# Feed-forward down projection by seven products of halves with weight low parts made by an adding DMA, and gate and up sums chained in PSUM

## The chip, the cores and the metric

The kernel runs on one core of a Trainium2 chip. The metric is the device time of one execution in microseconds (us); several executions are timed and their median is quoted. One execution is recorded by the hardware profiler, and the trace of it is what all rows below come from. Engine names are those of the profile: PE is the matrix engine, PEld its weight loads, DVE the vector engine, ACT the scalar engine, POOL the GpSimd engine, SP the engine that issues the loads.

## The reference, cut to what matters

One encoder layer over 512 tokens of width 1024: a feed-forward block (FFN1), attention and a short convolution with a combined input and an output projection, a second feed-forward block of the same shape (FFN2), and a gated embedding at the end. The change touches the two feed-forward blocks only. All values are float32.

```python
def swiglu(x, wg, wu, wd):
    return (jax.nn.silu(x @ wg) * (x @ wu)) @ wd
...
x = layer_norm(DN_ALPHA * x + 0.5 * swiglu(x, ffn1_wg[i], ffn1_wu[i], ffn1_wd[i]), ln1_g[i], ln1_b[i])
...
x = layer_norm(DN_ALPHA * x + 0.5 * swiglu(x, ffn2_wg[i], ffn2_wu[i], ffn2_wd[i]), ln3_g[i], ln3_b[i])
```

x is 512 x 1024, wg and wu are 1024 x 2816, wd is 2816 x 1024.

## The kernel before, in words

**Products of float32.** Each operand is held as two fp32r tiles, a high part (a rounding cast on ACT, L111) and a low part (the operand less its high part, a subtraction on DVE, L112); `split` makes both. A product is three matmul passes, high by high, high by low, low by high (`PASSES`), each recorded at L132 in `mm`. `unit` (L114) loads a 512 KB block of weights by an SP DMA into a page and splits it.

**Tiling of an FFN** (`ffn`, L239). The 2816 hidden columns are 22 chunks of 128. They are taken in groups of 4, 4, 4, 4 and 6 chunks. For each group the gate and up products of its chunks are computed, then silu(gate) x up (silu on ACT L329, product on DVE L330, into a tile hf), then the group's part of the down projection is added into `nat`, the 512 x 1024 result, four tiles of 128 tokens.

**Gate and up.** The first two chunks of an FFN go through `plain`. All others go two chunks at a time through `two` (L302): the 1024 x 256 block of each of wg and wu and the tokens are cut in halves, and seven products of halves (of sums of quarters: S1 to S4 of the weights, made by `weights` on DVE at L286, L287, L292, L293; T1 to T4 of the tokens, made once) give what eight would. Each of the seven products is 24 matmuls of 256 columns into a PSUM bank of its own (gate and up side by side, 512 columns). They are combined outside PSUM: one copy on ACT (L333) and seven sums of 512 columns on DVE (L334 to L342). `put_chunk` makes silu, hf and the split of hf for each of the two chunks.

**Down projection of a four-chunk group** (L389 to L399). For each of two column halves, four PSUM banks, one for each block of 128 tokens, take 4 chunks x 3 passes of 128 x 512; 96 matmuls in all. wd comes in four 512 KB blocks by `unit`. Eight `scalar_tensor_tensor` of 512 columns on DVE (L399) add the banks into `nat`. The last group of six chunks (L373 to L388) also does the layer norm; its form is left as it is by the change.

**What sets the order.** Each engine runs its instructions in one fixed order, made by a scheduler from the program order and from priorities: code under `tc.high_priority(offset=n)` is moved n places ahead. The offset is 25 for the first chunks of FFN1 and 100 for later ones, 400 and 50 in FFN2, 125 and 0 for wd. Working tiles live in a ring of 38 pages of 512 KB, handed out first freed, first reused (`page`, `free`); a tile that is written into a reused page waits for the last reader of the page's former tile. There are eight PSUM banks, handed out in turn.

## Time and profile before

| | us |
|---|---|
| median of three runs | 1027.2 |
| the three runs | 1023.98, 1028.66, 1027.2 |
| the profiled execution | 1026.09 |
| its span in the trace | 1024.0 |

The profiled execution is 1.1 us under the median and inside the three runs; its span leaves out 2.1 us at its two ends. Its mean granted clock of PE is 0.998 of full speed. FFN1 runs from about 11 to 320 us of the span and FFN2 from about 630 to 936 us; a four-chunk group takes 62 us. The rows below are of this execution: busy time of an engine is the union of its instructions, and an instruction's own duration is longer than the distance to the next one where they run back to back.

### The profile page before, as it was taken

To read this page: it belongs to the slowest core of one execution; us is meant where nothing else is said; L and a number is where in the kernel's file an instruction comes from. 1 tells how busy PE (TensorE), PEld (TensorE's weight loads), DVE (VectorE), ACT (ScalarE), POOL (GpSimd) and SP (SyncE) were. 2 spreads that over 40 slices of the span, in tenths; PEclk is the share of its full clock that TensorE was granted. 3 is DMA by queue.
4 is the path that set the end of the run, shared out by engine and by line. 5 is a ranking of instruction groups with operands and counts; after the bars stand their busy time and mean duration, and the time that the engine had idled before them with its cause. 6 is when DMAs were issued, how large, how long until landed. Compare 5 with 4: busy or idle time off the path is not lost.

```text
span 1024.0 us, 15507 instructions
## 1 busy us (share of the span) xinstructions
PE 1004.6 (98%) x6313; PEld 903.8 (88%) x6313; DVE 822.2 (80%) x1283; ACT 441.8 (43%) x621; POOL 25.0 (2%) x35
## 2 busy tenths in 40 slices
PE   8999999999999999999999999999999999999998
PEld 7989999898998878888878778989999898998787
DVE  7897868978697958999479988896868969689852
ACT  6444424433354235332576836443425324246221
POOL 1000000000000200000000011000000000000100
PEclk9999999999999999999999999999999999999999
DMA  9342324323335231424013223331424322227111
GB/s 311 122 123 83 109 98 131 97 83 107 100 119 185 69 92 42 128 58 124 20 42 104 83 65 101 124 124 39 127 83 144 103 79 87 83 85 265 52 41 51
DMA packets 99510, 104.57 MB, mean 102 GB/s; under 512 B 5872, under 2 KB 81904, under 8 KB 99440
## 3 DMA queue, kind: packets, MB, share of 16 engines
q1 hardware_dynamic: 99440, 103.60, 31.8%
q8 instruction: 49, 0.80, 0.3%
q14 instruction: 21, 0.17, 0.1%
HBM read 101.49 MB, written 2.10 MB: 101 GB/s over the span
## 4 chain that ended last, share of the span: by engine, by line
PE 89%; DMA 4%; DVE 3%; ACT 3%; issue 1%; POOLq 0%; SPq 0%; ACTq 0%
PE bk L132 86%; ACT pg L111 2%; DVE pg L112 1%; DMA pg<-in_ffn_wu_dram 1%; PE bk L506 1%; DMA pg<-in_w_in_dram 1%; DMA pg<-in_x_t_dram 1%; PE bk L507 1%; PE bk L704 1%; DMA pg<-in_ple_proj_w_dram 1%; DMA pg<-in_ffn_wd_dram 0%; PE bk L146 0%; ACT a L676 0%; DMA pg<-in_ple_gate_w_dram 0%; PE bk L692 0%
## 5 line engine op out<-in xcount | busy, mean ns | idle before, releaser
L132 PE MATMUL bk<-pg,pg 128*128 128x256 f32 (+1 forms) x2832 | 496.4, 333 | 4.4 <-ACT pg L111 1.8
L132 PEld LDWEIGHTS bk<-pg,pg 128*128 128x128 f32 x2832 | 427.6, 190 | 56.0 <-ACT pg L111 2.6
L111 ACT CAST pg<-pg 128x1024 fp32r<-128x1024 f32 (+1 forms) x267 | 260.0, 984 | 313.3 <-PE bk L132 78.4
L112 DVE TENSOR_TENSOR pg<-pg,pg 128x1024 fp32r<-128x1024 f32 (+1 forms) x267 | 300.6, 1139 | 40.6 <-ACT pg L111 35.5
L132 PE MATMUL bk<-xq,pg 128*128 128x256 f32 x2208 | 275.3, 284 | 4.6 <-DVE mv L158 1.5
L132 PEld LDWEIGHTS bk<-xq,pg 128*128 128x128 f32 x2208 | 270.6, 193 | 7.0 <-ACT pg L111 2.3
L132 PE MATMUL bk<-xT,pg 128*128 128x512 f32 (+2 forms) x600 | 133.0, 381 | 0.3 <-ACT xT L111 0.2
L132 PEld LDWEIGHTS bk<-xT,pg 128*128 128x128 f32 (+1 forms) x600 | 109.9, 186 | 21.5 <-ACT xT L111 0.5
L132 PE MATMUL bk<-pg,xT 128*128 128x512 f32 (+1 forms) x312 | 69.5, 374 | 1.3 <-DVE nat L385 1.3
L132 PEld LDWEIGHTS bk<-pg,xT 128*128 128x128 f32 x312 | 55.0, 188 | 11.4 <-ACT pg L111 1.8
L329 ACT ACTIVATE a<-pg 128x512 f32<-128x512 f32 x40 | 25.2, 629 | 71.7 <-DVE pg L338 66.1
L111 ACT CAST pg<-hf 128x512 fp32r<-128x512 f32 (+1 forms) x56 | 34.6, 618 | 35.2 <-DVE hf L330 19.6
L112 DVE TENSOR_TENSOR pg<-hf,pg 128x512 fp32r<-128x512 f32 (+1 forms) x56 | 38.3, 684 | 4.7 <-ACT pg L111 4.5
L399 DVE SCALAR_TENSOR_TENSOR nat<-bk,nat 128x512 f32<-128x512 f32 x64 | 40.4, 682 | 0.8 <-PE bk L132 0.7
L330 DVE TENSOR_TENSOR hf<-a,pg 128x512 f32<-128x512 f32 x40 | 27.5, 688 | 13.6 <-ACT a L329 13.5
L338 DVE TENSOR_TENSOR pg<-bk,pg 128x512 f32<-128x512 f32 x20 | 13.8, 692 | 29.9 <-PE bk L132 29.4
L160 POOL TENSOR_TENSOR mv<-mv,mhalf 128x1 f32<-128x1 f32 x12 | 17.8, 1480 | 627.0 <-DVE mv L159 627.0
L286 DVE TENSOR_TENSOR pg<-pg,pg 128x512 f32<-128x512 f32 x40 | 27.3, 686 | 5.7 <-DMA pg<-in_ffn_wg_dram 5.7
L292 DVE TENSOR_TENSOR pg<-pg 128x512 f32<-128x512 f32 x40 | 27.4, 686 | 2.9 <-PE bk L132 2.9
L112 DVE TENSOR_TENSOR pg<-bk,pg 128x512 fp32r<-128x512 f32 (+2 forms) x37 | 22.5, 626 | 8.5 <-ACT pg L111 8.1
L287 DVE TENSOR_TENSOR pg<-pg,pg 128x512 f32<-128x512 f32 x40 | 27.3, 685 | 0.0
L293 DVE TENSOR_TENSOR pg<-pg,pg 128x512 f32<-128x512 f32 x40 | 27.1, 686 | 0.1
(100 smaller groups left out, 612.7 us busy)
## 6 DMA issues: line engine op xcount, KB each, us to landing
pg<-in_ffn_wg_dram SPq DMA_DIRECT2D x44, 512.0 KB, 4.1
pg<-in_ffn_wu_dram SPq DMA_DIRECT2D x44, 512.0 KB, 4.7
pg<-in_ffn_wd_dram SPq DMA_DIRECT2D x44, 512.0 KB, 4.0
pg<-in_w_in_dram SPq DMA_DIRECT2D x28, 512.0 KB, 3.6
pg<-in_w_out_dram SPq DMA_DIRECT2D x8, 512.0 KB, 3.9
pg<-in_ple_gate_w_dram SPq DMA_DIRECT2D x8, 512.0 KB, 4.8
pg<-in_x_t_dram SPq DMA_DIRECT2D x4, 512.0 KB, 7.5
nat<-in_x_dram SPq DMA_DIRECT2D x4, 512.0 KB, 8.9
```

The costliest lines, as they stand in the source:

```text
L111: nc.scalar.copy(hi, src)
L112: nc.vector.tensor_sub(lo, src, hi.bitcast(F32))
L132: nc.tensor.matmul(ps, lhsT=st[a], rhs=mv[b], start=first and i == 0 and k == 0, stop=last and i == n - 1 and k == 2)
L160: nc.gpsimd.tensor_tensor(mv[:, 3:4], mv[:, 2:3], mhalf, op=ALU.pow)
L286: nc.vector.tensor_add(S1, A21, A22)
L287: nc.vector.tensor_sub(S2, S1, A11)
L292: nc.vector.tensor_sub(S3, A11, A21)
L293: nc.vector.tensor_sub(S4, A12, S2)
L329: nc.scalar.activation(s_t, e[m][:, :, 0], AF.Silu)
L330: nc.vector.tensor_mul(h3, s_t, e[m][:, :, 1])
L338: nc.vector.tensor_add(e[0][:, 1], prod("S4", "B22"), u4)
L399: nc.vector.scalar_tensor_tensor(dst, acc[t], CY, dst, op0=ALU.mult, op1=ALU.add)
```

## The change

Three things change, for the eight four-chunk groups (four in each FFN) and, for the second, for all twenty calls of `two`.

1. **Down projection by seven products** (`down7`). The hidden values of a pair of chunks are cut in halves by chunk and by tokens (256 columns), wd by chunk and by columns (512). `pair_ops` makes the four sums of quarters of the hidden values on DVE (four operations of 256 columns) and splits three of the four quarters (768 columns) and the sums (1024 columns) into high and low parts; the silu products are written straight into the tile `pair` and no longer split one by one. `diff` makes four sums of wd quarters (T1 to T4, 1024 columns each, DVE). Seven products over two token blocks, two pairs and three passes are 84 matmuls of 128 x 512. They go into three pairs of banks X, Y, Z; several products are summed in one bank, and each stage of a bank is added into `nat` by `put_out`, 14 operations of 512 columns a group.
2. **Weight parts** (`parts`). The high part of each of the seven wd operands is a cast on ACT. The low part is no longer a subtraction on DVE: ACT writes the operand times -1, rounded to fp32r, and a DMA issued by POOL adds the operand to it in place, 512 KB each. Loads of wd, parts and differences have priority 200 in both FFNs.
3. **Gate and up sums in PSUM** (`two`). The products are chained in three banks: b1 takes A11, then S2, S3 and A22 products on top, b2 takes A12, b3 takes S1, then S4. ACT copies the stages of b1 to SBUF (four copies of 512 columns), and three DVE sums remain.

```diff
@@ -248,7 +249,117 @@
+        SLOT = {"A12": 0, "A22": 1, "A11": 2, "A21": 3, "S1": 0, "S2": 1, "S3": 2, "S4": 3}
+        def raw_of(pair, m):
+            return pair[:, 2 - 2 * m:4 - 2 * m]
+        def pair_ops(pair):
+            A12, A22, A11, A21 = (pair[:, i] for i in range(4))
+            a = page([P, 4, 256]), page([P, 4, 256])
+            split(a[0][:, :3], a[1][:, :3], pair[:, :3])
+            s_ = page([P, 4, 256], F32)
+            nc.vector.tensor_add(s_[:, 0], A21, A22)
+            nc.vector.tensor_sub(s_[:, 1], s_[:, 0], A11)
+            nc.vector.tensor_sub(s_[:, 2], A11, A21)
+            nc.vector.tensor_sub(s_[:, 3], A12, s_[:, 1])
+            sums = page([P, 4, 256]), page([P, 4, 256])
+            split(*sums, s_)
+            free(pair, s_)
+            return a, sums
+        def down7(f0, pairs):
+            w4 = wd[f0 * P:(f0 + 4) * P].rearrange("(i k p) n -> k p i n", k=2, p=P)
+            hp = lambda: tc.high_priority(offset=AHEAD_W)
...
+            B11, B12, B21, B22 = (raw[i] for i in ((0, 0), (0, 1), (1, 0), (1, 1)))
+            def parts(src):
+                hi, lo = page([P, 2, 512]), page([P, 2, 512])
+                nc.scalar.copy(hi, src)
+                nc.scalar.mul(lo, src, -1.0)
+                nc.gpsimd.dma_start(lo, src, accum_op=ALU.add)
+                return hi, lo
+            def diff(a, b):
+                t = page([P, 2, 512], F32)
+                nc.vector.tensor_sub(t, a, b)
+                return t
+            def product(banks, a, w, first):
+                for b in range(2):
+                    for i, (q, sums) in enumerate(pairs):
+                        st = sums if a[0] == "S" else q
+                        for n, (x_, y_) in enumerate(PASSES):
+                            nc.tensor.matmul(banks[b], lhsT=st[x_][:, SLOT[a], ts(b)], rhs=w[y_][:, i],
+                                             start=first and i == 0 and n == 0, stop=i == 1 and n == 2,
+                                             skip_group_check=not first)
+            def put_out(banks, m, n):
+                for b in range(2):
+                    dst = nat[2 * m + b][:, n * 512:(n + 1) * 512]
+                    nc.vector.scalar_tensor_tensor(dst, banks[b], CY, dst, op0=ALU.mult, op1=ALU.add)
+            X_, Y_, Z_ = ([bank("all") for _ in range(2)] for _ in range(3))
+            with hp():
+                w = parts(B11)
+            product(X_, "A11", w, True)
+            put_out(X_, 0, 0)
+            free(*w)
...
+            with hp():
+                T1 = diff(B12, B11)
+                w = parts(T1)
+                free(B11)
+            product(Y_, "S1", w, True)
+            put_out(Y_, 1, 1)
+            free(*w)
...
@@ -299,7 +408,7 @@
+            def product(ps, a, b, first):
                 for i, (nm, _) in enumerate(mats):
-                    mm(ps[:, i], [((W[nm][a][0][:, c], W[nm][a][1][:, c]), (X.q[b][0][:, c], X.q[b][1][:, c])) for c in range(4)])
+                    for c in range(4):
+                        for k, (x_, y_) in enumerate(PASSES):
+                            nc.tensor.matmul(ps[:, i], lhsT=W[nm][a][x_][:, c], rhs=X.q[b][y_][:, c],
+                                             start=first and i == 0 and c == 0 and k == 0,
+                                             stop=i == 1 and c == 3 and k == 2, skip_group_check=not first)
                 return ps
...
-            nc.scalar.copy(p1, prod("A11", "B11"))
-            nc.vector.tensor_add(e[0][:, 0], prod("A12", "B21"), p1)
-            nc.vector.tensor_add(u2, prod("S2", "T2"), p1)
-            p5 = prod("S1", "T1")
-            nc.vector.tensor_add(u4, p5, u2)
-            nc.vector.tensor_add(e[0][:, 1], prod("S4", "B22"), u4)
+            b1, b2, b3 = bank2(), bank2(), bank2()
+            nc.scalar.copy(p1, product(b1, "A11", "B11", True))
+            nc.vector.tensor_add(e[0][:, 0], product(b2, "A12", "B21", True), p1)
+            nc.scalar.copy(u2, product(b1, "S2", "T2", False))
+            product(b3, "S1", "T1", True)
+            nc.scalar.copy(u3, product(b1, "S3", "T3", False))
+            nc.vector.tensor_add(e[1][:, 1], b3, u3)
+            nc.vector.tensor_add(e[0][:, 1], product(b3, "S4", "B22", False), u2)
             put_chunk(0)
-            nc.vector.tensor_add(u3, prod("S3", "T3"), u2)
-            nc.vector.tensor_add(e[1][:, 1], p5, u3)
-            nc.vector.tensor_add(e[1][:, 0], prod("A22", "T4"), u3)
+            nc.scalar.copy(e[1][:, 0], product(b1, "A22", "T4", False))
             put_chunk(1)
...
@@ -386,18 +503,9 @@
             else:
-                for half in range(2):
-                    acc = [bank("all") for _ in range(NTB)]
-                    for i in range(per):
-                        wv = wd_rows(i, half)
-                        for t in range(NTB):
-                            mm(acc[t], [(both(h[i], ts(t)), wv)], first=i == 0, last=i == per - 1)
-                        free(*held[i, half])
-                    for t in range(NTB):
-                        dst = nat[t][:, half * 512:(half + 1) * 512]
-                        nc.vector.scalar_tensor_tensor(dst, acc[t], CY, dst, op0=ALU.mult, op1=ALU.add)
-            free(*h)
+                down7(f0, h[::2])
```

The places left out are the loads of the four quarters of wd, five more products of the same form in `down7`, and the callers.

**How it moves instructions.** The rows are the engines' orders in the third group of FFN1 (`[waits X]` is a wait on engine or queue X; DMAHW are queues of loads, DMASW those of POOL's DMAs). First ACT of the kernel before, from the copy of the second `two` of the group to the split of its third chunk: pg17, pg16 and pg31 are high parts of wd, pg13 and pg2 those of hf.

```order
L333 COPY pg14_188_1691<-bk_49_1693 128x512 [waits PE_49]
L329 ACTIVATE a_9_1633<-pg35_159_1439 128x512 [waits DVE_49]
L111 CAST pg17_193_1896<-pg7_192_1894 128x1024 [waits DMAHW5_49]
L111 CAST pg16_199_1964<-pg32_198_1962 128x1024 [waits DMAHW6_49]
L111 CAST pg13_163_1636<-hf_9_1632 128x512 [waits DVE_49]
L111 CAST pg31_202_1994<-pg10_201_1992 128x1024 [waits DMAHW7_49]
L329 ACTIVATE a_10_1824<-pg8_186_1689 128x512 [waits DVE_49,Activation_49]
L111 CAST pg2_190_1827<-hf_10_1823 128x512 [waits DVE_49]
```

Now ACT at the same place after the change, from the middle of the second `two` to the cast of the second pair's three quarters (the last row). L289 and L291 are the high part and the times -1 of `parts`, L441 silu, L453 the last copy of bank b1.

```order
L289 CAST pg12_251_2035<-pg0_250_2033 128x1024 [waits DVE_49]
L289 CAST pg27_245_1993<-pg10_244_1991 128x1024 [waits PE_49]
L291 ACTIVATE pg9_246_1994<-pg10_244_1991 128x1024 [waits PE_49]
L289 CAST pg28_248_2014<-pg5_247_2012 128x1024 [waits PE_49]
L291 ACTIVATE pg20_249_2015<-pg5_247_2012 128x1024 [waits PE_49]
L291 ACTIVATE pg30_252_2036<-pg0_250_2033 128x1024
L289 CAST pg32_253_2054<-pg36_239_1945 128x1024 [waits DMAHW7_49]
L441 ACTIVATE a_10_1895<-pg31_227_1738 128x512 [waits DVE_49]
L453 COPY pg29_228_1739<-bk_29_1742 128x512
L441 ACTIVATE a_11_1923<-pg29_228_1739 128x512 [waits Activation_49]
L291 ACTIVATE pg31_254_2055<-pg36_239_1945 128x1024 [waits DVE_49]
L112 CAST pg35_231_1926<-pg13_204_1687 128x768 [waits DVE_49]
```

Two wd casts of 1024 columns stood between a silu and the next cast that the matmuls read; now there are eight operations of `parts` among these twelve, two more of them right ahead, all in front of the cast of the second pair.

PE of the kernel before, from the last matmul of gate and up into the down projection: bk_56 to bk_59 are its first four banks.

```order
L132 MATMUL bk_55_1857<-pg26_26_355,pg3_177_1666 128x256
L132 MATMUL bk_56_1890<-pg17_193_1896,pg0_162_1576 128x512 [waits PE_49,Activation_49]
L132 MATMUL bk_56_1890<-pg30_194_1897,pg0_162_1576 128x512 [waits DVE_49]
L132 MATMUL bk_56_1890<-pg17_193_1896,pg0_162_1576 128x512
L132 MATMUL bk_57_1891<-pg17_193_1896,pg0_162_1576 128x512 [waits PE_49]
L132 MATMUL bk_57_1891<-pg30_194_1897,pg0_162_1576 128x512
```

PE after the change, inside the down projection of the same group, from the first S1 product to the first A11 matmul of the second pair (pg35, the tile that the last ACT row above writes).

```order
L305 MATMUL bk_34_1949<-pg27_245_1993,pg11_202_1683 128x512 [waits Activation_49]
L305 MATMUL bk_35_1950<-pg27_245_1993,pg11_202_1683 128x512
L305 MATMUL bk_34_1949<-pg9_246_1994,pg11_202_1683 128x512 [waits DMASW0_49]
L305 MATMUL bk_34_1949<-pg27_245_1993,pg19_203_1684 128x512
L305 MATMUL bk_35_1950<-pg9_246_1994,pg11_202_1683 128x512
L305 MATMUL bk_35_1950<-pg27_245_1993,pg19_203_1684 128x512
L305 MATMUL bk_37_1952<-pg17_242_1972,pg8_199_1674 128x512 [waits PE_49,Activation_49]
L305 MATMUL bk_37_1952<-pg1_243_1973,pg8_199_1674 128x512
L305 MATMUL bk_37_1952<-pg17_242_1972,pg33_200_1675 128x512
L305 MATMUL bk_32_1947<-pg4_240_1953,pg35_231_1926 128x512 [waits Activation_49]
```

Before, a down projection began when both chunks' splits were there and waited on ACT and DVE at its head; now its matmuls wait for ACT's parts, for the adding DMAs (DMASW), for a bank that ACT copies out, and for the second pair's cast.

## Rows read from the trace of the kernel before

**Rows 1.** The page's busy times by engine, share of the span, instructions.
```profile
PE 1004.6 (98%) x6313; PEld 903.8 (88%) x6313; DVE 822.2 (80%) x1283; ACT 441.8 (43%) x621; POOL 25.0 (2%) x35
```

**Rows 2.** The chain that ended last: start us, us, engine, tile, line, count.
```profile
11.04 308.99 PE bk L132 x2219
629.88 305.84 PE bk L132 x2201
```

**Rows 3.** Three group lengths of FFN1: busy by engine, clock, DMA share, GB/s.
```profile
core 0: us, PE busy (x) PEld busy (x) DVE busy (x) ACT busy (x) POOL busy (x), PEclk, DMA share, GB/s
62.00:124.00 62.00, 62.00 (x433) 58.26 (x432) 50.70 (x69) 24.93 (x31) 0.00 (x0) 1.00 0.32 102
124.00:186.00 62.00, 62.00 (x434) 58.23 (x433) 48.72 (x65) 24.50 (x30) 0.00 (x0) 1.00 0.31 103
186.00:248.00 62.00, 62.00 (x433) 58.27 (x432) 50.31 (x69) 24.73 (x31) 0.00 (x0) 1.00 0.31 102
```

**Rows 4.** PE's timeline into the first down projection: start us, us, instructions.
```profile
42.75 5.92 PE L132 MATMUL bk<-xq,pg 128*128 128x256 f32 x48
48.51 27.71 PE L132 MATMUL bk<-pg,pg 128*128 128x256 f32 x144
76.06 4.12 PE L132 MATMUL bk<-xq,pg 128*128 128x256 f32 x33
```

**Rows 5.** Groups by line and form: count, busy us, mean ns, idle before.
```profile
L112 DVE TENSOR_TENSOR pg<-pg,pg 128x1024 fp32r<-128x1024 f32 x226 | 273.5, 1221 | 37.7 <-ACT pg L111 33.0 <-ACT a L329 2.7 <-PE bk L132 1.7
L111 ACT CAST pg<-pg 128x1024 fp32r<-128x1024 f32 x226 | 235.8, 1050 | 270.3 <-PE bk L132 63.4 <-DVE pg L287 56.4 <-DMA pg<-in_ffn_wd_dram 47.3
L399 DVE SCALAR_TENSOR_TENSOR nat<-bk,nat 128x512 f32<-128x512 f32 x64 | 40.4, 682 | 0.8 <-PE bk L132 0.7
L330 DVE TENSOR_TENSOR hf<-a,pg 128x512 f32<-128x512 f32 x40 | 27.5, 688 | 13.6 <-ACT a L329 13.5
L329 ACT ACTIVATE a<-pg 128x512 f32<-128x512 f32 x40 | 25.2, 629 | 71.7 <-DVE pg L338 66.1 <-DVE pg L342 5.6
L333 ACT COPY pg<-bk 128x512 f32<-128x512 f32 x20 | 11.7, 586 | 14.7 <-PE bk L132 14.6
L112 DVE TENSOR_TENSOR pg<-bk,pg 128x256 fp32r<-128x256 f32 x8 | 3.3, 414 | 0.0
```

**Rows 6.** ACT's timeline in the fourth group of FFN1, columns as in rows 4.
```profile
225.12 0.63 ACT L329 ACTIVATE a<-pg 128x512 f32<-128x512 f32 x1 [0.16 <-DVE pg L342]
225.65 2.02 ACT L111 CAST pg<-pg 128x1024 fp32r<-128x1024 f32 x2
227.57 0.62 ACT L111 CAST pg<-hf 128x512 fp32r<-128x512 f32 x1
```

**Rows 7.** DVE's timeline in the same group, columns as in rows 4.
```profile
229.86 2.35 DVE L112 TENSOR_TENSOR pg<-pg,pg 128x1024 fp32r<-128x1024 f32 x2
...
254.42 1.28 DVE L399 SCALAR_TENSOR_TENSOR nat<-bk,nat 128x512 f32<-128x512 f32 x2
255.68 1.23 DVE L112 TENSOR_TENSOR pg<-pg,pg 128x1024 fp32r<-128x1024 f32 x1
```

**Rows 8.** DMA issues: count, KB each, median us from issue to landing.
```profile
pg<-in_ffn_wd_dram SPq DMA_DIRECT2D x44, 512.0 KB, 4.0
...
nat<-in_x_dram SPq DMA_DIRECT2D x4, 512.0 KB, 8.9
out_dram<-hf SPq DMA_DIRECT2D x7, 256.0 KB, 2.0
```

**Rows 9.** DMA queues: packets, MB, share of 16 engines.
```profile
q1 hardware_dynamic: 99440, 103.60, 31.8%
```

**Rows 10.** A stretch in which PE waits, columns as in rows 3.
```profile
328.00:330.00 2.00, 0.98 (x6) 0.48 (x4) 1.29 (x2) 1.89 (x3) 0.76 (x1) 1.00 0.00 0
```

**Rows 11.** POOL's costliest group, columns as in rows 5.
```profile
L160 POOL TENSOR_TENSOR mv<-mv,mhalf 128x1 f32<-128x1 f32 x12 | 17.8, 1480 | 627.0 <-DVE mv L159 627.0
```

More of the change, by code (lines that the diff above doesn't have):

```diff
@@ L37 @@
 AHEAD_D2 = 0
+AHEAD_W = 200
 NEMB = 2
@@ L262, in plain @@
                 free(*u)
-            hf = ring("hf", 2, [P, 512])
             s_t = ring("a", 2, [P, 512])
             nc.scalar.activation(s_t, ps["g"], AF.Silu)
-            nc.vector.tensor_mul(hf, s_t, ps["u"])
-            return put(hf)
+            nc.vector.tensor_mul(hf, s_t.rearrange("p (a b) -> p a b", a=2), ps["u"].rearrange("p (a b) -> p a b", a=2))
         def weights(w, fc, ops, pages):
@@ L300, in weights, with two @@
             yield
-        def two(fc, ah):
+        def two(fc, ah, place):
             W, pages = {nm: {} for nm, _ in mats}, []
@@ L320, in two, with bank2 @@
+            def bank2():
+                return bank("all").rearrange("p (m n) -> p m n", m=2)
             e = [page([P, 2, 2, 256], F32) for _ in range(2)]
             k = [page([P, 2, 2, 256], F32) for _ in range(2)]
-            p1, u2, u3, u4 = k[0][:, 0], k[0][:, 1], k[1][:, 0], k[1][:, 1]
-            h = []
+            p1, u2, u3 = k[0][:, 0], k[0][:, 1], k[1][:, 0]
             def put_chunk(m):
-                hf = ring("hf", 2, [P, 512])
-                h3 = hf.rearrange("p (a b) -> p a b", a=2)
@@ L352, in ffn @@
                 fc = f0 + len(h)
+                if last:
+                    hf = [ring("hf", 2, [P, 2, 256]) for _ in range(2)]
+                    two(fc, ahead_f, lambda m: hf[m])
+                    h += [put(z.rearrange("p a b -> p (a b)")) for z in hf]
+                    continue
+                pair = page([P, 4, 256], F32)
                 if fc < nplain:
-                    h.append(plain(fc, first if fc == 0 else {}, 2, ahead))
-                    if len(h) == nplain:
-                        free(*X.q["B12"])
-                        X.sums()
-                else:
-                    h += two(fc, ahead if fc < 4 else ahead_f)
+                    for m in range(2):
+                        plain(fc + m, first if fc + m == 0 else {}, 2, ahead, raw_of(pair, m))
+                    free(*X.q["B12"])
+                    X.sums()
+                else:
+                    two(fc, ahead if fc < 4 else ahead_f, lambda m: raw_of(pair, m))
+                h += [pair_ops(pair), None]
             wds, held = {}, {}
```

48 lines of the change are left out of this document (42 added, 6 removed).

## The prediction

> **What bounds the kernel now.** I read first the busy times [rows 1], then the chain of work that ended last [rows 2], then windows of one four-chunk group each [rows 3]. PE is busy for 98% of the span, and the chain runs without a break on PE's matmuls through either FFN (309.0 and 305.8 us); in a group PE has no idle time, while DVE is busy 49.9 us of 62 (mean of the three windows) and ACT 24.7. So fewer matmuls shorten the FFNs if, and only if, the operands keep arriving as early as PE can use them. The reader is to see in rows 3 that ACT has room on average; what follows turns on where in the group its work stands.
>
> **Rates.** From PE's timeline [rows 4]: 48 matmuls of 256 columns start 5.76 us apart from the next row, 0.120 us each; the following 144 take 27.55 us, of which 48 are again of 256 columns, so one of 512 columns costs (27.55 - 5.76) / 96 = 0.227 us. An instruction lasts longer than it holds up the next: two ACT casts of 1024 columns take 2.02 us where one takes 1.05 [rows 5, 6], so 0.97 apart; silu 0.53 apart from what follows [rows 6]. On DVE 1024 columns are 1.13 apart (2.35 for two) and 512 are 0.60 apart (1.28 for two) [rows 7]. Estimates on the same lines: a PSUM copy of 512 on ACT (0.586 long) 0.49 apart, 768 columns 0.74 on ACT and 0.87 on DVE, 256 columns (0.414 long) 0.33 on DVE.
>
> **What PE saves.** Per group 96 matmuls of 512 columns become 84: 12 x 0.227 = 2.72 us. Eight groups: 21.8 us. Gate and up keep their matmuls; chaining in PSUM takes none away.
>
> **What DVE does.** Per group: minus 8 sums (two calls of `two`, 4 fewer each), minus 4 low parts of hf (both 0.60), minus 4 low parts of wd (1.13), plus 4 differences of wd (1.13), plus twice (0.87 + 4 x 0.33 + 1.13 = 3.32) for `pair_ops`, plus 6 put-outs (0.60): -4.8 - 2.4 - 4.5 + 4.5 + 6.6 + 3.6 = +3.0, so 52.9 of a group that could last 62.1 - 2.7 = 59.4 us. Tighter, not a bound.
>
> **What ACT does.** Minus 4 casts of wd (3.9), minus 4 of hf (2.1), plus 6 PSUM copies (2.9), plus 14 operations of `parts` (13.6), plus twice a cast of 768 and one of 1024 (3.4): +13.9, so 38.6 of 59.4 us. Not a bound on average either. But the 13.6 us of `parts` come in one run, with the casts that PE waits for behind them.
>
> **The run on ACT, FFN1.** In the order after the change, 14 ACT operations lead to the cast of the second pair's hidden quarters: nine of `parts`, silu, copy, silu, one more of `parts`, the cast. The first may start only when a matmul late in the S4 product has released its page, and the first A11 matmul of the second pair waits for the last. ACT needs 9 x 0.97 + 0.53 + 0.49 + 0.53 + 0.97 + 0.84 = 12.1 us for them. PE has in that stretch 37 matmuls of 256 and 16 of 512 columns, 4.4 + 3.6 = 8.1 us. The difference, 4.0, less up to 0.6 that PE waits inside the stretch anyway, is 3.4 to 4.0 us of idle PE that nothing hides; I take 3.5. The other waits of a group are smaller. The A22 product continues bank b1 only when ACT has copied out the stage before, and that copy stands behind the cast of the sums, which waits for four DVE operations: 0 to 2.2 us, I take 0.6. The S4 product takes bank b3 only after DVE's add, which needs that same copy: 0.6. Later products of `down7` take a bank only after its put-outs (0.68 long [rows 5], and queued behind others on DVE): 1.0 for four such hand-offs. Sum 5.7 a group. Were operations to hold up the next for their full length, the same walk gives 10.5.
>
> **The adding DMA.** No row of before has a DMA on POOL's queue, or one from SBUF to SBUF: the one queue that carries data is that of the loads [rows 9]. The nearest rows are the loads: 4.0 us for wd's 512 KB, 8.9 for the slowest 512 KB, 2.0 for 256 KB [rows 8]. I take 4.0, as the same bytes, with 2.0 and 8.9 as ends; none is a gain, since the low part was made by one DVE operation (1.22). In FFN1 the matmul that waits for T1's DMA loses nothing below 5.5 us, because PE waits for the ACT run behind it anyway. Traffic adds 7 x 0.52 MB a group to some 6.3 MB (102 GB/s x 62 us) at a DMA share of 0.31 [rows 3]: room enough.
>
> **The run on ACT, FFN2.** Gate and up have priority 50 there, `parts` 200, but the loads come later, so `parts` begin after the last gate and up matmul. Walked from there: copy, silu, high part of B21 (PE waits 1.3), its times -1, cast of the second pair (1.3), cast of its sums, high part of T1 (1.0), then two matmuls that wait for B21's and T1's DMAs (0.8 each at 4.0 us; 0 at 2.0; together 6.4 at 8.9): 5.2 us. A load that is issued just in time for its cast costs 1.7 ahead of it, the bank hand-offs 1.0. Sum 8 a group.
>
> A rule bears on this price. The Trainium skill, "DMA: Bandwidth & Descriptors", section "Anatomy of one DMA — SWDGE (gpsimd) path", gives a fixed 2.0 us and the bytes at 436 GB/s for a DMA issued by GpSimd; an estimate from that page is 3.2 us, which would take about 5 us off FFN2's waits. No run here shows it yet.
>
> **Sum.** The profiled execution took 1026.1 us: 1026.1 - 21.8 + 4 x 5.7 + 4 x 8 = 1059. It lies 1.1 under the median, inside the spread of the runs, so I do not correct for that. Nothing outside the FFNs changes in work; the last groups keep their matmuls, and their calls of `two` have DVE sums fewer, worth nothing while PE is the bound. PE's clock I leave as it is: where PE waited in before, the granted clock stayed at 1.00 [rows 10], the 2.4 GHz level.
>
> **Rivals.**
> A. *PE stays the bound.* ACT has 21 us of room in a group, and the pages may come free earlier than my walk has it, so that the run of `parts` slides ahead under gate and up. Then the waits stay small, under 0.4 us a group: 1026.1 - 21.8 + 3 = 1007. For it: ACT 43% busy [rows 1] and most of its idle time spent waiting for loads, PE and DVE [rows 5]. Against it: the order is fixed, and a page release by a matmul stands in front of the run.
> B. *The waits eat the saving exactly.* Only the ACT run in FFN1 and half of FFN2's costs, 2.7 us a group on average: 1026.
> C. *The adding DMA is slow.* If it lands after 8.9 us [rows 8], FFN1 loses 3.4 more a group and FFN2 about 4.8 more: 1059 + 4 x 3.4 + 4 x 4.8 = 1092. It decides from 5.5 us on. The mechanism would be that POOL gets its DMAs out late while DVE, busy 50 us of 62 [rows 3], is at work; POOL's one small operation on a 128 x 1 tile takes 1.48 us [rows 11], so POOL is not quick at anything. The same figure comes out if ACT's operations do not overlap: FFN1 at 10.5 a group instead of 5.7 and FFN2 at 12 gives 1094. A rule of the Trainium skill speaks for C: "SBUF — State Buffer", section "Who interferes with whom", has a DVE operation in a two-port mode lock out descriptor writing, and a tensor_tensor of two SBUF inputs contend with GpSimd's reads; this kernel's DVE is mostly the latter, which the page clears of blocking descriptors; no run here shows either.
> That the change does not do what it says is left out: PE's order has the 84 matmuls.
>
> **How the numbers follow.** Chances: forecast 0.50, A 0.18, B 0.10, C 0.22. The forecast's own range is 1036 to 1076: FFN1 waits of 4 to 8 a group, FFN2 of 4 to 10. A lies at 1004 to 1020, C at 1076 to 1110. For 8 in 10 I leave out most of A below and the far end of C above: 1012 to 1098. What can be told from no change is 0.5%, about 5 us. Faster is A: 0.18. Within 0.5% is B: 0.10. Slower is the forecast and C: 0.72.
>
> **What would show it.** In the windows of a group PE's busy time would fall to about 59.4 us while the group takes 65 in FFN1 and 67 in FFN2, with ACT at 38 to 39 us of it. In the chain, PE's long stretches break into pieces, with ACT's L289, L291 and L112 between them, and DMA of POOL's queue in FFN2. The idle time ahead of `down7`'s matmuls names ACT as releaser; some 12 us of back-to-back ACT ends in the cast of 768 columns and the first matmul of the second pair starts right after. The DMA list would give the adding DMA's time, 3 to 5 us. Wrong would be: L291 and L289 spread out under gate and up with PE busy throughout (A), or DMASW named as the releaser in FFN1 as well (C), or waits at places that my walk does not name, at loads or at pages.

## The result and the profile after

The changed kernel takes 1163.8 us (median of four runs, 1159.3 to 1172.4) against 1027.1 us before: ratio 1.1345, 95% interval 1.1274 to 1.1416. The prediction was 1059 us, within 1012 to 1098: the direction came out, the size did not, by 105 us. Every one of the four runs lies outside the range. The profiled execution is the 1172.4 us one (span 1170.6 us), and sums on its rows are made against that span.

The page's busy times by engine, as in [rows 1]:

```profile
PE 1047.1 (89%) x6217; PEld 912.5 (78%) x6217; DVE 842.3 (72%) x1315; ACT 558.1 (48%) x761; POOL 75.4 (6%) x91
```

Two things are to be seen. PE is idle for 1170.6 - 1047.1 = 123.5 us, where it was 19.4: **104 us more idle**. And PE is busy for longer, though it has 96 matmuls fewer: at the rate of [rows 4] its busy time should be 1004.6 - 21.8 = 982.8, so **64 us more** for the same work. 104 + 64 - 22 = 146, the whole difference of the spans (146.6). Most of the 64 is clock: the stretches of this trace in which the granted clock was 0.50 add up to 119.9 us, PE was busy in 91.9 of them, and half of that, 46 us, is what the lower clock cost its work (1.7 us in the kernel before). The other 18 us or so are not clock; e3 below has 10.5 us more of busy time with the mean clock at 0.997, against 0.998 before. What PE waited for, all over the program (us in total, times, the longest):

```profile
PE bk L305 <- DMA pg<-pg: 44.9, 18, 4.4
PE bk L305 <- DVE nat L312: 38.2, 9, 7.3
PE bk L426 <- ACT pg L449: 7.4, 9, 3.3
PE bk L426 <- ACT pg L445: 4.9, 5, 2.7
...
PE bk L426 <- DVE pg L450: 2.2, 2, 2.0
PE bk L305 <- ACT pg L112: 2.1, 5, 0.5
```

The adding DMA comes first, the put-outs of `down7` next, the hand-offs of the chained banks third (7.4 + 4.9 + 2.2 = 14.5 us), and the ACT run on which the prediction built is last (2.1 us). Two whole groups of FFN1 and two of FFN2, each from one down projection to the next, columns as in [rows 3]:

```profile
137.04:209.19 72.15, 64.65 (x423) 58.42 (x421) 53.16 (x73) 37.98 (x46) 6.07 (x7) 0.95 0.55 137
209.19:284.32 75.13, 64.73 (x422) 57.86 (x421) 53.04 (x73) 38.08 (x47) 6.08 (x7) 0.95 0.54 134
732.77:816.34 83.57, 67.58 (x420) 59.54 (x420) 53.27 (x72) 38.54 (x46) 6.15 (x7) 0.87 0.48 120
816.34:898.65 82.31, 68.50 (x420) 60.45 (x420) 53.39 (x72) 38.52 (x46) 6.15 (x7) 0.87 0.49 122
```

A group lasts 72 and 75 us in FFN1 and 84 and 82 in FFN2, where 65 and 67 were forecast. DVE's 53 us and ACT's 38 are what the prediction counted (52.9 and 38.6); PE's 65 to 68 are not (59.4). The granted clock, 1.00 in all of [rows 3], is 0.95 and 0.87 here. PE's timeline in the first down projection of FFN2, with the wait before each piece:

```profile
732.77 2.98 PE L305 MATMUL bk<-pg,pg 128*128 128x512 f32 x6 [4.21 <-DMA pg<-pg]
736.21 3.12 PE L305 MATMUL bk<-pg,pg 128*128 128x512 f32 x6 [0.46 <-ACT pg L112]
743.12 9.75 PE L305 MATMUL bk<-pg,pg 128*128 128x512 f32 x34 [3.80 <-DMA pg<-pg]
760.20 7.45 PE L305 MATMUL bk<-pg,pg 128*128 128x512 f32 x24 [7.33 <-DVE nat L312]
```

The six matmuls after 736.21 take about 0.5 us each, twice the 0.227 of before: the 1.2 GHz level. The 34 after the wait of 3.80 us take 9.75 us, where 34 x 0.227 = 7.7 would do; the 24 after the wait of 7.33 us take 7.45 instead of 5.4. Both lose 2.0 us, a short wait as much as a long one.

Where the 7.33 us come from is seen on DVE and SP. DVE in the same stretch, then the two waits of SP from 725 to 760 us that bear on it, and the load they lead to:

```profile
749.28 0.69 DVE L312 SCALAR_TENSOR_TENSOR nat<-bk,nat 128x512 f32<-128x512 f32 x1 [0.43 <-PE bk L305]
758.17 0.69 DVE L395 TENSOR_TENSOR pg<-pg,pg 128x512 f32<-128x512 f32 x1 [8.19 <-DMA pg<-in_ffn_wg_dram]
758.77 1.28 DVE L312 SCALAR_TENSOR_TENSOR nat<-bk,nat 128x512 f32<-128x512 f32 x2
```
```profile
SPq L383 <- DMA pg<-pg: 11.4, 2, 6.6
SPq L383 <- PE bk L305: 5.7, 2, 4.8
```
```profile
747.67 0.37 SPq L383 DMA_DIRECT2D pg<-in_ffn_wg_dram  x1
```

The put-outs that PE needs (758.77) stand on DVE behind a sum of the next chunk's weights (L395), which waits 8.19 us for their load. SP issued that load only at 747.67: it had waited for its page, 6.6 us for an adding DMA and then for the matmuls of `down7` behind it. The load then took some 10 us to land, against a median of 4.9 (4.1 before). So a late adding DMA reaches PE twice, once by its result and once by a page that is free late. Over the whole trace SP's loads of gate and up have 60.0 us of waits that an adding DMA ends, in eight waits:

```profile
SPq L383 <- DMA pg<-pg: 60.0, 8, 13.7
```

The DMA issues (as in [rows 8]) and the queues that carry data (as in [rows 9]):

```profile
pg<-pg POOLq DMA_DIRECT2D x56, 512.0 KB, 6.8
```
```profile
q1 hardware_dynamic: 99440, 103.60, 28.0%
q0 software_dynamic: 8064, 29.36, 13.8%
```

### The profile page after: what moved, and what is told of

It reads as the page before. It is cut to its first block, busy times and chain, and to the rows that moved or that the text cites. A ratio compares the mean times of both kernels' runs of the same rounds, so it can differ in the third digit from the quotient of the medians.

```text
span 1170.6 us, 15663 instructions
## 1 busy us (share of the span) xinstructions
PE 1047.1 (89%) x6217; PEld 912.5 (78%) x6217; DVE 842.3 (72%) x1315; ACT 558.1 (48%) x761; POOL 75.4 (6%) x91
## 3 DMA queue, kind: packets, MB, share of 16 engines
q1 hardware_dynamic: 99440, 103.60, 28.0%
q0 software_dynamic: 8064, 29.36, 13.8%
## 5 line engine op out<-in xcount | busy, mean ns | idle before, releaser
L112 ACT CAST pg<-pg 128x1024 fp32r<-128x1024 f32 (+2 forms) x267 | 253.9, 970 | 320.4 <-DMA pg<-in_ffn_wg_dram 75.9
L305 PE MATMUL bk<-pg,pg 128*128 128x512 f32 x672 | 203.5, 457 | 85.9 <-DMA pg<-pg 44.9
L426 PE MATMUL bk<-pg,pg 128*128 128x256 f32 x1440 | 192.4, 287 | 12.3 <-ACT pg L449 7.4
L133 PE MATMUL bk<-pg,pg 128*128 128x512 f32 (+1 forms) x624 | 143.7, 378 | 4.5 <-ACT pg L112 2.2
L312 DVE SCALAR_TENSOR_TENSOR nat<-bk,nat 128x512 f32<-128x512 f32 x112 | 74.0, 683 | 23.7 <-PE bk L305 23.6
L292 POOL DMA_DIRECT2D pg<-pg x56 | 49.1, 876 | 556.5 <-ACT pg L291 419.9
L289 ACT CAST pg<-pg 128x1024 fp32r<-128x1024 f32 x56 | 58.0, 1041 | 41.4 <-DMA pg<-in_ffn_wd_dram 17.7
L291 ACT ACTIVATE pg<-pg 128x1024 fp32r<-128x1024 f32 x56 | 58.3, 1052 | 12.5 <-PE bk L426 7.8
L395 DVE TENSOR_TENSOR pg<-pg,pg 128x512 f32<-128x512 f32 x40 | 27.4, 686 | 37.1 <-DMA pg<-in_ffn_wg_dram 30.2
L297 DVE TENSOR_TENSOR pg<-pg,pg 128x1024 f32<-128x1024 f32 x32 | 38.3, 1220 | 20.5 <-DMA pg<-in_ffn_wd_dram 20.3
```

What stands on the lines that cost most here:

```text
L112: nc.scalar.copy(hi, src)
L133: nc.tensor.matmul(ps, lhsT=st[a], rhs=mv[b], start=first and i == 0 and k == 0, stop=last and i == n - 1 and k == 2)
L289: nc.scalar.copy(hi, src)
L291: nc.scalar.mul(lo, src, -1.0)
L292: nc.gpsimd.dma_start(lo, src, accum_op=ALU.add)
L297: nc.vector.tensor_sub(t, a, b)
```

## The experiments

Times are medians of four runs each; PE's idle and busy time are those of each profiled span. The profile numbers lines by each kernel, so `two`'s and `down7`'s lines move by a few. Every edit gives each engine a new order of instructions, beside what it is meant to change.

| kernel | us | ratio to before, 95% | PE idle | PE busy | DVE busy |
|---|---|---|---|---|---|
| before | 1027 | | 19.4 | 1004.6 | 822 |
| changed | 1163.8 | 1.127 to 1.142 | 123.5 | 1047.1 | 842 |
| e1 low parts by DVE | 1106.2 | 1.075 to 1.080 | 77.5 | 1029.8 | 903 |
| e2 same, ACT's work kept | 1117.3 | 1.085 to 1.093 | 83.7 | 1030.6 | 904 |
| e3 chaining alone | 1040.5 | 1.011 to 1.017 | 29.2 | 1015.1 | 774 |
| e4 put-outs first | 1162.3 | 1.129 to 1.134 | 119.1 | 1041.6 | 843 |
| e5 e1 with filling matmuls | 1106.9 | 1.073 to 1.082 | 56.3 | 1044.0 | 903 |
| e6 e1, gate and up chain first | 1126.1 | 1.093 to 1.099 | 95.1 | 1030.4 | 902 |
| e7 parts left out | 1143.6 | 1.108 to 1.116 | 102.6 | 1040.1 | 841 |
| e8 priority 400 | 1165.4 | 1.130 to 1.138 | 120.1 | 1046.4 | 843 |
| e9 e1 with adding DMAs beside | 1251.3 | 1.216 to 1.224 | 178.6 | 1067.7 | 907 |
| e10 changed with filling matmuls | 1157.5 | 1.125 to 1.131 | 96.6 | 1058.5 | 842 |
| e11 seven products alone, parts by DVE | 1110.0 | 1.077 to 1.088 | 81.0 | 1022.2 | 950 |
| e12 before, with a longer ACT chain | 1112.6 | 1.081 to 1.088 | 84.4 | 1025.8 | 827 |
| e13 e1 delayed by a pair | 1157.5 | 1.120 to 1.131 | 111.4 | 1042.9 | 905 |
| e14 e11 delayed by a pair | 1110.5 | 1.073 to 1.085 | 79.8 | 1027.0 | 950 |
| e15 changed, delayed by a pair | 1219.0 | 1.179 to 1.190 | 147.7 | 1066.9 | 845 |
| e16 e1, 8 of 14 put-outs left out | 1075.9 | 1.043 to 1.046 | 59.9 | 1014.0 | 865 |
| e17 e1, differences left out | 1075.2 | 1.040 to 1.047 | 60.0 | 1013.2 | 868 |
| e18 both left out | 1056.6 | 1.024 to 1.029 | 48.1 | 1010.5 | 829 |

**The adding DMA and ACT's part of it (e1, e2).** In `parts`, e1 has the three lines with minus replaced by a split on ACT and DVE; e2 keeps the cast and the ACT product and only replaces the DMA by a subtraction on DVE:

```diff
 # e1
-                nc.scalar.copy(hi, src)
-                nc.scalar.mul(lo, src, -1.0)
-                nc.gpsimd.dma_start(lo, src, accum_op=ALU.add)
+                split(hi, lo, src)
 # e2
-                nc.gpsimd.dma_start(lo, src, accum_op=ALU.add)
+                nc.vector.tensor_sub(lo, src, hi.bitcast(F32))
```

> The changed kernel with the low parts of wd made by one DVE subtraction again (the seven ACT products with -1 and the seven adding DMAs of a group are gone, everything else stands). Theory D (the adding DMA, 6.8 us from issue to landing, starts the loss: PE waits for it 45 us in all, the pages it reads come free late, so the next weight loads and DVE's put-outs behind them are late, 38 us, and the waits pull PE's clock to 0.949, some 64 us): nearly all of that goes, 1163.8 less 45, 30 and 45, about 1045, clock 0.98 or more. Theory A (the run of ACT operations is the cause): the run is half as long too, so about the same time; this run alone does not tell D from A. Theory P (the bank hand-offs of the products chained in PSUM are the cause): still above 1120.

> As the run before, but ACT still writes the operand times -1 into the low part and DVE then writes the low part over it, so ACT keeps all 14 operations of a group and only the adding DMA is gone. Theory D: within 15 us of the run before (1045 to 1060), since the DMA is the cause. Theory A: ACT's run costs PE the 3.5 to 5 us a group that the prediction gave it, so 30 to 45 us above the run before. Theory P: above 1120.

e1 took 1106.2, not 1045; e2 11 us more, 1117.3. So of 1163.8 - 1106.2 = 57.6 us, 11 go with ACT's seven products a group and 46.5 with the DMA, net of the DVE subtraction that stands in its place (61 us of DVE time in all). Theory D names a large part rightly and is wrong about "nearly all": 79 us over before remain with no adding DMA in the kernel. Theory A asked for 30 to 45 us between e2 and e1, and theory P for more than 1120; both fall.

**Chaining in PSUM (e3, e11).** e3 is the kernel before with the new `product` and sums in `two`; e11 is e1 with the old ones.

> The kernel before with only the sums of gate and up changed: products chained in three PSUM banks, four ACT copies and three DVE sums; the down projection is the old one with 96 matmuls. Theory D: the chaining costs only the hand-offs that the changed kernel's trace shows between ACT's copies, DVE's sum and PE (14.5 us in 16 waits), so 1035 to 1045. Theory P: these waits and the clock they pull down make up a large part of the loss, 1070 or more. If the hand-offs hide behind other matmuls: 1027.

> The seven products of the down projection with low parts by DVE and the old sums of gate and up (one copy, seven DVE sums, a bank for each product). If chaining costs here what it costs alone (e3: 13.5 us), 1093. If it costs more inside the changed kernel, since its copies stand on ACT beside the parts of wd: 1060 to 1080. If DVE is the bound by now (eight more sums a group, some 4.8 us on a DVE that is at 59 us of 70): 1110 or more.

Alone the chaining costs 13.5 us, inside what theory D forecast, and takes 49 us of work off DVE (822 to 774) that nobody was waiting for. That the hand-offs in the changed trace add up to about the same is partly chance: in e3's own profiled execution, the slowest of its four, ACT's copies of the banks hold PE up for 6.4 us only, and PE is busy 10.5 us longer at a clock of 0.997. With the seven products the chaining makes no difference that is clear of noise (e11's runs 1105.7 to 1117.0, e1's 1104.7 to 1109.3). e11 lies at the edge of the branch that it named for DVE as the bound; PE waits 20.6 us there for the gate and up sums on DVE. That the chaining's waits and its DVE time cancel is a reading, not shown.

**The order of put-outs and the start of the parts (e4, e8).**

```diff
 # e4, in put_out
+                with tc.high_priority(offset=200):
                     for b in range(2):
 # e8
-AHEAD_W = 200
+AHEAD_W = 400
```

> The changed kernel with the 14 put-outs of a group moved ahead in priority, so that on DVE they stand before the next chunks' weight operations, which wait for loads. If the 38 us that PE waits for put-outs come from this place in DVE's queue, these waits fall under 10 us and the time to 1110 or 1130 (some of the clock comes back with them). If it is the lateness of the loads itself, PE waits instead for the next weights, and the time stays within 10 us of 1164.

> The changed kernel with the loads, differences and parts of wd at priority 400 instead of 200. If the adding DMAs hurt because they start too late, PE's 45 us of waits for them halve and the time falls to 1120 or less. If pages and loads allow no earlier start, the order moves little and the time stays within 15 us of 1164; more pages held early may also delay the gate and up loads, up to 1190.

Neither helps: 1162.3 and 1165.4. In e4 the waits for put-outs fall from 38.2 to 33.0 us, and those for ACT's casts rise to 11.0; in FFN2's groups the weight sum still stands ahead of put-outs in DVE's order, so the run does not settle what put-outs that stand first would bring. e8 came in as its second branch had it: the lateness of the loads was not cured by priority.

**What a wait costs in clock (e5, e10, e12).** e5 and e10 put matmuls that nobody reads just ahead of a matmul that waits; e12 lengthens ACT's chain in the kernel before.

```diff
 # e5 (n = 18) and e10 (n = 16), in product, before the second pair's first matmul
+                        if a == "A11" and b == 0 and i == 1:
+                            fill(n)   # n matmuls of 128 x 512 into a free bank
 # e12, in put, 24 times for a four-chunk group's last chunk
+            for _ in range(extra):
+                nc.scalar.copy(ht[:, 0], hf)
```

> The kernel of e1 (low parts by DVE, 1106 us) with 18 more matmuls of 128 x 512 in each four-chunk group, whose result nobody reads: they stand on PE just ahead of the second pair's first matmul, where e1's trace shows waits of 4.0 and 4.3 us for ACT's cast, and write a bank that comes free with DVE's last gate and up sum. Theory K (each long wait also lowers PE's granted clock for the work behind it; in e1 PE is busy 47 us longer than its matmuls took at the clock of before): 8 x 18 x 0.227 = 32.7 us of useless work fill waits that are there anyway, the clock rises from 0.975 to 0.985 or more, and the time falls by 10 to 25 us. Rival (the longer busy time has another cause, such as slower operand reads): the time stays or grows by up to 15 us and the clock does not rise.

> The changed kernel with 16 matmuls of 128 x 512 a group whose result nobody reads, just ahead of or among the first pair's matmuls that wait for the adding DMA: 8 x 16 x 0.227 = 29 us of useless work at full clock. Theory K (waits pull the granted clock down): the clock rises from 0.949 to 0.97 or more and the time stays within 10 us of 1164 or falls to 1145, since the work lies in waits and the matmuls behind run faster. Rival (the clock falls for another reason): 1180 to 1195 with the clock unchanged.

> The kernel before with 24 more ACT copies of 512 columns ahead of the high part of each four-chunk group's last hidden chunk, each of which writes what the cast then writes over: a longer chain on ACT that PE has to wait for, with nothing else changed. Theory K: PE's idle time grows by some us a group, and PE's busy time grows beside it although its matmuls are the same, by half to the whole of the idle time, the clock falling under 0.99. Rival: only the idle time grows, PE's busy time stays at 1005 us. If the longer chain stays under the 36 matmuls of the first three chunks (8.2 us), the time does not change and the run tells nothing.

In e5, 32.7 us of useless work changed nothing (1106.9 against 1106.2). The clock, 0.975 to 0.984 in e1's four runs, is 0.989 to 0.996 in e5's. In the profiled executions (the slowest of e1's, the fastest of e5's) PE's idle time falls by 21.2 us, and its busy time without the filling is 1044.0 - 32.7 = 1011.3, 18.5 less than in e1. In e10 the clock is 0.969 to 0.971 where the changed kernel had 0.949 to 0.956, and with 29 us more work the kernel is not slower (1155.9 to 1159.3 against 1159.3 to 1172.4). e12's matmuls are those of before, and PE is busy 21 us longer beside 65 us of waits. Three of its waits, in PE's timeline:

```profile
81.23 7.24 PE L132 MATMUL bk<-pg,pg 128*128 128x512 f32 x24 [9.30 <-ACT pg L111]
152.97 7.21 PE L132 MATMUL bk<-pg,pg 128*128 128x512 f32 x24 [7.84 <-ACT pg L111]
225.57 8.38 PE L132 MATMUL bk<-pg,pg 128*128 128x512 f32 x24 [8.73 <-ACT pg L111]
```

24 x 0.227 = 5.4; the waits cost 1.8, 1.8 and 2.9 us behind them. Half of PE's busy time at the granted clock of 0.50 is 20.7 us in e12 and 1.7 in the kernel before, so the clock makes 19 of the 21. Theory K's mechanism, that a long wait lowers the clock of the work behind it, holds in all three, in FFN code with and without the change. Its sizes did not all hold: e5's time was to fall by 10 to 25 us and stayed, since the filling cost what the clock gave back, and e12's busy time was to grow by half of the idle time or more and grew by a third.

**Result or page (e9).** e1 with one more line in `parts`: the adding DMA runs into a scratch page.

```diff
                 split(hi, lo, src)
+                nc.gpsimd.dma_start(beside, src, accum_op=ALU.add)
```

> The kernel of e1 (low parts by DVE, used by the products) with the seven adding DMAs of a group running beside it: each adds the same operand into one scratch page that nobody reads. PE never waits for them, but they hold the operand's page, POOL's queue and the DMA engines as in the changed kernel. If the adding DMA hurts by PE's direct waits: within 10 us of e1's 1106. If it hurts by what it holds (pages released late, loads late, put-outs behind them on DVE): 1130 to 1150, with PE waiting for weights and put-outs.

1251.3 us, 145 more than e1 and 100 over the upper branch, with a DMA for whose result PE does not wait. The page for e9, and the waits that tell why:

```profile
PE 1067.7 (86%) x6217; PEld 923.9 (74%) x6217; DVE 906.8 (73%) x1373; ACT 508.4 (41%) x705; POOL 73.2 (6%) x91
```
```profile
ACT pg L112 <- DMA pg<-pg: 59.6, 7, 12.0
POOL pg L293 <- DMA pg<-pg: 180.1, 34, 8.6
```

ACT waits for a page that an adding DMA still reads, up to 12.0 us a time. The size is not that of the changed kernel: into one scratch page the DMAs run one after another (POOL's line), so they hold their operands longer. That holding pages is enough to cost time, without any wait of PE for the result, is shown; how much of the changed kernel's loss it makes is not. The loads themselves are not slower in e9 (medians of 4.1, 4.8 and 4.0 us for wg, wu and wd, as before); in the changed kernel they are (4.9, 5.4 and 4.8, against 3.8, 4.2 and 4.2 in e1).

**The parts, and the chain to the second pair (e6, e7, e13 to e15).** e6 gives the operations from `two`'s products to `pair_ops` priority 400. e7 keeps one pair of parts in each FFN. e13 to e15 call `down7` one pair of chunks later:

```diff
             while len(h) < per:
+                if len(h) == 2 and pending:
+                    down7(*pending.pop())
...
-                down7(f0, h[::2])
+                pending.append((f0, h[::2]))
```

> The kernel of e1 with the copies, sums, silu, products and quarter sums of gate and up ahead in priority (400 against 200 for the parts of wd), so that on ACT and DVE the chain from the last gate and up matmul to the second pair's cast stands before the parts of wd. Theory Q (what remains in e1 is queueing of this chain behind parts of wd, as in its trace 2.4 us of two low parts on DVE and 1.0 us of a cast on ACT): PE's 27 us of waits for ACT's casts fall by half or more and some clock comes back, 1106 to 1070 or 1085. Rival S (the length of the chain itself, with only the first pair's 18 matmuls to cover it): within 10 us of 1106.

> The changed kernel with wd's parts made once in each FFN and used for all its products (54 of the 56 pairs of parts, with their ACT operations and adding DMAs, are left out, the differences and loads stay; the result is that of other weights). What is left is the shape of the seven products, their banks, put-outs and the hidden sums. Theory D with Q (supply of the parts is the cause): close to what PE needs, 1010 to 1035. Rival S (the shape: pairs that must be complete, banks that must be put out between two products): 1060 or more.

> The kernel of e1 (seven products, low parts by DVE, sums chained) with each four-chunk group's down projection written one step later, behind the first pair of chunks of the next group, so that the chain from its last gate and up matmul to the second pair's operands, and wd's parts, lie under 168 matmuls of the next group. Theory S (what is left in e1 is the shape: products that need both pairs, with 18 matmuls to cover the second pair's chain): PE's 27 us of waits for that cast and most of the clock loss go, 1106 to 1030 or 1060. Theory O (many short waits of the fixed orders, wherever the products stand): within 15 us of 1106.

> The same delay with the old sums of gate and up (the kernel of e11 delayed). Theory S: as the run before, 1030 to 1060, and below it if the bank hand-offs of the chaining show once the rest is covered (13.5 us alone). If DVE, which does eight sums more a group, is the bound once PE's waits are covered: above the run before.

> The changed kernel itself with the same delay: adding DMAs as they are. Theory D in its narrow form (PE's direct wait for the DMA is the cost): covered too, within 15 us of e13. In its wide form (the DMA holds the operand's page, so that the next loads and what stands behind them come late, as e9 has it): 40 us or more above e13.

e6, e13 and e14 missed both of their branches: e6 is 20 us slower than e1, and the delay changes nothing in e14 and costs 51 us in e13. e7, at 1143.6 with almost no parts to make, came in on the side of rival S (1060 or more), which e13 and e14 then did not bear out. In each the waits do not go, they come up elsewhere: in e13 PE waits 23.9 us for put-outs, 17.1 for gate and up casts and 14.1 for the pair's casts. In e7 it waits for gate and up operands as well, 28.2 us against 5.6 in e1:

```profile
PE bk L424 <- ACT pg L112: 19.4, 9, 4.8
PE bk L424 <- DVE pg L113: 8.8, 7, 4.8
```

Theories Q and S both fall as they were stated. e15 lies 62 us above e13, the number that theory D's wide form gave. It does not speak for that form, though, for the delay did not cover PE's direct waits for the DMA; they are longer than in the changed kernel (44.9):

```profile
PE bk L305 <- DMA pg<-pg: 51.2, 24, 4.9
```

**How much DVE has to do (e16 to e18).** e16 drops the put-outs of A11, S1, S2 and S3; e17 uses plain quarters in place of T1 to T4.

```diff
 # e16, likewise (Y_, 1, 1), (X_, 0, 1), (X_, 1, 1)
-            put_out(X_, 0, 0)
 # e17, likewise T2 = B22, T3 = B12, T4 = B21
-                T1 = diff(B12, B11)
+                T1 = B12
```

> The kernel of e1 with 8 of a group's 14 put-outs left out (those between two products of one bank; the products go on adding in the bank, so the result is another). PE need not wait for a bank between the products S1 and S4, and A11, S2, S3 and A22, and DVE has 8 x 0.6 = 4.8 us less a group. If the hand-off of a bank to DVE and back, with DVE's queue in it, is a main part of what e1 lost (its trace names DVE's put-outs for 6.8 us only, but they push other work on DVE back): 1106 to 1070 or below. If put-outs are only the named 6.8 us: 1095 to 1102.

> The kernel of e1 with the four differences of wd quarters left out in each group (each product takes a plain quarter instead, so the result is another). DVE has 4 x 1.13 = 4.5 us less a group, about as much as in e16, and the parts of wd no longer wait for one another; banks and put-outs stay. If what matters is how much DVE has to do around the down projection: as far down as e16. If it is the banks: within 10 us of 1106.

> Both left out: DVE has 9.3 us less a group. If the two are separate costs, the sum of the two falls; if both are DVE's load, the second brings less than alone. If 1106 hardly moves, the loss of e1 lies on ACT and the operands' chain, not on DVE.

Two different cuts of about the same DVE time (38 and 36 us of 903) bring about the same, 30.3 and 30.9 us; both together 74 us of DVE time and 49.6 us. e16's freer banks are worth no more than e17's fewer differences. That fits DVE's load better than the banks, but does not show it: e16 takes away the waits for put-outs (6.8 us in e1), e17 some of those for the second pair's cast (27.1 to 18.5 us), and both leave out work that the result needs. PE's longest waits in e16 are for ACT's cast of the second pair as before (26.0 us); that cast ends a chain which passes DVE twice. In e1 it was seen so (DVE, where the sum L448 and the product L439 stand behind low parts):

```profile
131.36 2.36 DVE L113 TENSOR_TENSOR pg<-pg,pg 128x1024 fp32r<-128x1024 f32 x2 [1.13 <-ACT pg L112]
133.64 0.68 DVE L448 TENSOR_TENSOR pg<-bk,pg 128x512 f32<-128x512 f32 x1
135.43 1.22 DVE L113 TENSOR_TENSOR pg<-pg,pg 128x1024 fp32r<-128x1024 f32 x1 [1.11 <-ACT pg L112]
136.58 0.68 DVE L439 TENSOR_TENSOR pg<-a,pg 128x512 f32<-128x512 f32 x1
```

**What stays open.** Leaving out DVE work gave back 50 of e1's 79 us at most. DVE's load does not explain e7, which has as little DVE work as the changed kernel, almost no parts and still 1143.6 us; its order of instructions also changed in many places, and which of these costs it was not separated. e7 has e1's matmuls and less work on DVE and ACT, and takes 37 us more, so the order, with the reuse of pages that goes with it, is a rival of that size that no run took apart. The adding DMA's price is not settled by e1 alone either: taking it out brought 57.6 us there and 20 in e7, where the parts went with it. No version of the change came near the kernel before.

## Why the prediction was wrong, step by step

- **PE's saving** of 21.8 us held as a count and a rate: 84 matmuls a group, and full-clock pieces run at 0.12 and 0.227 us each. It is the one gain, and it is inside every sum above.
- **PE's clock "as it is"** failed, and it is the largest mis-sized term: 0 was put for 46 us. Some 18 us more of PE's busy time are not clock and had no term either; what they are was not separated. The row that the zero rested on [rows 10] had a wait of 1 us; the forecast had PE wait some 3.5 us at a time in FFN1 and up to 1.7 in FFN2, and did not ask what the clock does behind such waits. The kernel before had a row for it, at its start, where PE's first matmuls stop for 1.5, 0.8 and 0.9 us (columns as in [rows 3]; 15 matmuls in 3 us, then 27):

```profile
11.20:14.20 3.00, 3.00 (x15) 3.00 (x16) 2.66 (x3) 2.06 (x3) 0.00 (x0) 0.50 1.18 308
15.00:18.00 3.00, 3.00 (x27) 3.00 (x26) 3.00 (x4) 2.36 (x3) 0.00 (x0) 1.00 1.12 333
```

- **The adding DMA** was taken at 4.0 us from the loads; it takes 6.8 at the median, and each issue occupies POOL for 0.88 us. Its own decision point in FFN1, 5.5 us, was passed, and its sign, the DMA named as releaser in FFN1 too, came, so rival C was the right direction, at 1092. In FFN2 two waits of 0.8 us were forecast, for T1's and B21's DMAs; the trace has 3.80 for B21's and, in a place that the walk did not name, 4.21 for the first DMA of the group, which the first product A11 reads. The two issues on POOL, each right behind ACT's operand times -1:

```profile
726.46 0.93 POOL L292 DMA_DIRECT2D pg<-pg  x1 [41.11 <-ACT pg L291]
735.84 0.87 POOL L292 DMA_DIRECT2D pg<-pg  x1 [8.45 <-ACT pg L291]
```

The estimate from the Trainium skill ("DMA: Bandwidth & Descriptors", section "Anatomy of one DMA — SWDGE (gpsimd) path") was 3.2 us; the measurement decides, and it is twice that.
- **What the DMA holds** was left out. The prediction asked who waits for the result, and not who waits for the pages that the DMA reads and writes. A forecast of 1.0 us a group for put-outs became 38.2 / 8 = 4.8, by the chain page, load, weight sum on DVE, put-out behind it, PE. e9 shows that held pages cost time; that it was this chain in the changed kernel is read from its trace at 760.20 and argued for the rest, and e4 did not undo it.
- **The run on ACT** was there, but it was not what PE waited for. In the second group of FFN1 its last eleven operations stretch from 134.99 to 144.35 us, the end of the cast; PE had stopped in the same place for the adding DMA until 142.03, so the two waits lay over each other:

```profile
134.99 1.05 ACT L289 CAST pg<-pg 128x1024 fp32r<-128x1024 f32 x1 [2.23 <-PE bk L426]
143.53 0.82 ACT L112 CAST pg<-pg 128x768 fp32r<-128x768 f32 x1
```
```profile
142.03 13.12 PE L305 MATMUL bk<-pg,pg 128*128 128x512 f32 x49 [2.76 <-DMA pg<-pg]
```

PE's waits of `down7` for ACT's casts (L112 and L289) are 2.8 us in all, against 28 forecast for FFN1's and FFN2's groups. e2 puts the price of ACT's extra work at 11 us of time.
- **DVE at "+3.0, tighter, not a bound"** was right as a count (842 us against 822) and wrong as a judgement. DVE does not have to be full to hold PE up: it needs only to be busy, or to wait, when PE's next operand or bank is behind it. e16 and e17 take some 4.6 us of DVE a group and give back 3.8.
- **Rival C's mechanism**, POOL kept from issuing by DVE, did not show: POOL's 56 issues take 0.86 to 1.04 us each, whether DVE is busy or not. The slow part is from the issue to the landing, with several such DMAs and the loads in flight; in e9, where they run one at a time, the median is 4.6 us. The Trainium skill's page "SBUF — State Buffer" (section "Who interferes with whom") clears DVE's operations with two SBUF inputs of blocking descriptors, and the trace agrees, with 1.04 us for the longest issue.
- **The range** ended at 1098 because every rival shifted one term at a time. The waits (104 us of idle against 55) and the clock (46 against 0) go together and needed one rival that has both. Rival B's price also does not follow from its own words: the ACT run in FFN1 (3.5) and half of FFN2's 8 are 3.75 us a group on average, 1034 us and not 1026.

## What to carry to other kernels

A kernel whose matrix engine is busy 98% of the time has its operands arriving just in time; a change that takes 2% off the matmuls and makes their operands come by longer chains pays with waits, and each wait of some microseconds costs the clock behind it as well, so price every new wait of that kind as its length and 2 to 3 us more, as the rows here have it. When work is moved from an engine to a DMA, count two waits: the one for the result, and the one for the memory that the DMA holds until it has landed, down to the next load into that page and whatever stands behind it in an in-order queue. An average of free time on the supplying engines says little; look at what stands in front of the operand in each queue. Every edit also reorders the engines, and e7 took 37 us more than e1 with less work, so a difference of that size between two variants has no single cause until a trace shows the wait that went.

## What the runs showed of the hardware

- After waits of 3.8 to 9.3 us PE's matmuls of 512 columns run at about half speed (six in 2.98 us behind 4.21, in the changed kernel), the 1.2 GHz level, before they return to 0.227 us each; the loss behind a wait was 1.8 to 2.9 us, and no larger behind 9.30 us (1.8) than behind 3.80 (2.0). Matmuls that nobody reads, put into the wait, brought the clock of the same kernel from 0.975 to 0.984 up to 0.989 to 0.996.
- An adding DMA of 512 KB from SBUF to SBUF took 6.8 us from issue to landing at the median in the changed kernel (4.5 to 12.2) and 4.6 us in e9, where one waited for the other, and its issue occupied POOL for 0.88 us. Its queue moved 29.36 MB in 13.8% of 16 engines' 1170.6 us, 182 MB a millisecond; the loads' queue moved 103.60 MB in 28.0%, 316 in the same unit. Byte for byte the addition cost 1.7 times a load.
